# One turn of six raw weight tiles for all loads of the MLP, in place of two separate sets of three

## The chip, the cores and the metric

The kernel runs on one core of one Trainium2 chip. The metric is the device time of one execution in microseconds (us); lower is better. The core has a matrix engine (TensorE, PE in the rows; PEld is its weight load), three engines for elementwise work (VectorE or DVE, ScalarE or ACT, GpSimd or POOL), and SyncE (SP), which issues nearly all loads of this kernel in order from one queue.

## The reference

A two-layer decoder in float32 over 256 tokens, width 2048. Layer 1 is a sparse attention (an indexer picks 64 keys per query) and an MLP; layer 2 has a dilated-window attention over shared keys and values, and an MLP; a last RMSNorm follows. The part that this change touches most is the MLP, once in each layer:

```python
def sq_relu_mlp(h, w_up, w_down):      # w_up 2048 x 8192, w_down 8192 x 2048
    u = jax.nn.relu(h @ w_up)
    return (u * u) @ w_down
```

## The kernel before

Every float32 weight is used in two parts. `split` (line 188) makes them: ACT casts the raw block to a rounded high part `whi` (line 190), DVE subtracts to get the low part `wlo` (line 191), each 128x1024 in the MLP. A product is then three matmuls of 128x512 for each 128 rows (`mm3`, lines 194 to 196, or line 382 in `gemm`). There are five `whi` and five `wlo` buffers in the MLP.

The MLP walks over eight blocks of 1024 hidden columns, e = 0 to 7. `up(e)` computes a block of `h @ w_up`, `down(e)` adds that block's part of the second product to the residual. The order is up(0), up(1), down(0), up(2), down(1), and so on; "round e" below is up(e) with the down(e-1) behind it.

- `up(e)` multiplies most of the inner dimension by a scheme of seven products in place of eight (`seven`, line 720). It is called three times, and each call loads two raw tiles of 1 MB, `rx` and `ry`, that hold the blocks b11, b12 and b21, b22. A call is seven splits and four in-place DVE additions on the raw tiles (lines 719, 721, 723, 726: b11 = b12 - b11, b12 = b22 - b12, and so on). Line 721 is the first of the four that needs `ry`. `rx` is last read by the split of b12, `ry` by the split of b21, the last of the call. The rest of the inner dimension is two raw tiles, `rows[0]` and `rows[1]`, split in four ordinary products `plain(r, c)`: both of `rows[0]` are over in the middle of the second call of `seven`, those of `rows[1]` come at the end of the third call and behind it. Below, the three calls are the first, second and third seven, and the pair `rows` the plain rows.
- For e > 0 the plain rows are loaded behind the first seven's tiles; for e = 0 ahead of them.
- `down(e)` is two calls of `gemm`, each with four raw tiles of 1 MB: eight tiles, d0 to d7, two splits each.

So a round loads 16 tiles of 1 MB: six for the three sevens, two plain rows, eight of down. Before the change, the sevens' six take three buffers named `wx` (pool `mlp`), the other ten take three named `wraw` (pool `wp`, which also serves the attention stages). A tile takes the buffer of its pool and name that comes free first, and a buffer is free when its last reader is done. Each engine's order is written down when the kernel is built, by a scheduler that forecasts times; the loads stand on SP's one queue in that order, so one that waits for a buffer holds up those behind it. Between attention and MLP, `project` loads the output weights, and `add_forms` takes one such tile as scratch (`gx`) for each half.

Of the kernel before, what the change touches and what calls it, by code (L numbers as in the profile page):

```python
# [11 lines left out]
F32 = mybir.dt.float32  # L12
# [5 lines left out]
P = 128  # L18
SEQ = 256
NT = SEQ // P  # L20
D = 2048
KC = D // P
# [19 lines left out]
GW = 1024  # L42
# [9 lines left out]
X0 = 2  # L52
ARRIVE = 2

HI_BUFS, LO_BUFS = 4, 3
HI_MORE, LO_MORE, RAW_MORE = 1, 2, 3

Q_W = NH * HD
# [5 lines left out]
NSM = ID + IH  # L64
# [28 lines left out]
def yoco_kernel(ctx: ExitStack, tc: tile.TileContext, x, a_w_in, a_w_out, w_kv, b_w_q, b_w_out, w_up, w_down,  # L93
# [7 lines left out]
    wp = ctx.enter_context(tc.tile_pool(name="wp", bufs=3))  # L101
# [3 lines left out]
    pools = {}  # L105
# [20 lines left out]
    def b2(dt=F32):  # L126
        return wk.tile([P, 512], dt, name="b2" + ("r" if dt == F32R else ""), tag="b2", bufs=8)
# [7 lines left out]
    def side():  # L135
        return ps2.tile([P, HALF], F32, name="side")
# [51 lines left out]
    def split(hi, lo, src):  # L188

        nc.scalar.copy(hi, src)  # L190
        nc.vector.tensor_tensor(lo, src, hi.bitcast(F32), op=ALU.subtract)  # L191
# [6 lines left out]
    def mm_wide(acc, w_hi, w_lo, xk, first, last):  # L198

        def both():  # L200
            nc.tensor.matmul(acc, w_hi, xk.rearrange("p a t -> p (a t)"), start=first, stop=last)

        if not last:
            both()
        nc.tensor.matmul(acc[:, :SEQ], w_lo, xk[:, 0], start=False, stop=False)
        if last:
            both()
# [28 lines left out]
        lo = lo_of.tile([P, GW], F32R, name="wlo", bufs=LO_BUFS if lo_of is wp else LO_MORE)  # L236
        return hi, lo

    def pair_raw():
        return pools["mlp"].tile([P, 2, GW], F32, name="wx", bufs=RAW_MORE)  # L240

    def norm_transpose(c4, which):

# [40 lines left out]
    def add_forms(halves, half, which):  # L284
        n, plain, f = halves[half]

        def transposed(c, c2):
            pt = side().rearrange("p (c t) -> p c t", c=2)
            for j in range(2):
                cc = 2 * c2 + j  # L290
                for t in range(NT):
                    nc.tensor.transpose(pt[:, j, t * P:(t + 1) * P], h[t][c][:, cc * P:(cc + 1) * P], ident)
                g = which * KC + 4 * c + cc
                yield cc, pt[:, j, :], gT[:, g:g + 1]

        if plain is not None:
            for c in range(2):
                for cc, pt, g in transposed(2 * half + c, 1):
                    hi, lo = plain[:, 2 * c + cc - 2, 0, :], plain[:, 2 * c + cc - 2, 1, :]
                    nc.scalar.activation(hi, pt, AF.Copy, scale=g)  # L300
                    nc.vector.scalar_tensor_tensor(lo, pt, g, hi.bitcast(F32), op0=ALU.mult, op1=ALU.subtract)
        gx = pair_raw()[:, :, :n * SEQ].rearrange("p c (j t) -> p c j t", t=SEQ)
        for c in range(2):
            for c2 in range(n // 2):
                for cc, pt, g in transposed(2 * half + c, c2):
                    nc.scalar.activation(gx[:, c, cc], pt, AF.Copy, scale=g)
        a11, a21, a12, a22 = gx[:, 0, :, :P], gx[:, 0, :, P:], gx[:, 1, :, :P], gx[:, 1, :, P:]
        s1, s2, s3, s4 = (b2()[:, :n * P].rearrange("p (q t) -> p q t", t=P) for _ in range(4))
        nc.vector.tensor_tensor(s1, a21, a22, op=ALU.add)
        nc.vector.tensor_tensor(s2, a11, s1, op=ALU.subtract)  # L310
        nc.vector.tensor_tensor(s3, a11, a21, op=ALU.subtract)
        nc.vector.tensor_tensor(s4, a12, s2, op=ALU.add)
        for name, v in (("a11", a11), ("a12", a12), ("s4", s4), ("s1", s1), ("s3", s3), ("s2", s2), ("a22", a22)):
            split(f[name][:, :, 0], f[name][:, :, 1], v)
# [37 lines left out]
    def load_w(w, r0, nk, cols, width):  # L352

        n = len(cols) * width
        raw = wp.tile([P, 2, GW], F32, name="wraw", bufs=3).rearrange("p a b -> p (a b)")[:, :nk * n]
        raw = raw.rearrange("p (k c) -> p k c", k=nk)
        joined = all(c == cols[0] + i * width for i, c in enumerate(cols))
        for i, c in enumerate(cols[:1] if joined else cols):
            m = n if joined else width
            nc.sync.dma_start(raw[:, :, i * width:i * width + m],  # L360
                              w[r0:r0 + nk * P, c:c + m].rearrange("(k p) c -> p k c", p=P))
        return raw
# [69 lines left out]
    take_x(0, raw_x, 0, X0)  # L432
    stat = stat_of(xa)
    cols_qi = (COL_QI, COL_QI + HALF)
    raw_w = wp.tile([P, 2, GW], F32, name="wraw", bufs=3)
    for c in range(2):
        nc.sync.dma_start(raw_w[:, 0, c * HALF:(c + 1) * HALF], a_w_in[0, :P, cols_qi[c]:cols_qi[c] + HALF])
    take_x(0, raw_x, X0, 4)
# [21 lines left out]

    def index_keys():

        raw = wp.tile([P, 2, GW], F32, name="wraw", bufs=3).rearrange("p a b -> p (a b)")[:, :KC * NSM]
        nc.sync.dma_start(raw.rearrange("p (k n) -> p k n", n=NSM),
                          a_w_in[0, :, COL_KI:COL_KI + NSM].rearrange("(k p) c -> p k c", p=P))
        acc = ps.tile([P, HALF], F32, name="acc")[:NSM]
        per = KC // 2
        for k0 in range(0, KC, per):
            hi, lo = (b[:, :per * NSM] for b in hi_lo())
            split(hi, lo, raw[:, k0 * NSM:(k0 + per) * NSM])  # L470
            for k in range(k0, k0 + per):
                xk = xa[k // 4][:, k % 4]
                r = slice((k - k0) * NSM, (k - k0 + 1) * NSM)
                mm_wide(acc, hi[:, r], lo[:, r], xk, k == 0, k == KC - 1)
        both = sum_halves(acc)
        pt = side()
        for t in range(NT):
            nc.tensor.transpose(pt[:, t * P:t * P + NSM], both[:, t * P:(t + 1) * P], ident[:NSM, :NSM])
        rstd = st.inv()
        rk = wk.tile([P, NT], F32, name="rk", tag="rk", bufs=2)  # L480
        nc.vector.tensor_scalar(rk, rstd, -SCALE, None, op0=ALU.mult)
        rA.extend((rstd, rk))
        kps = side()
        for t in range(NT):
            r = rstd[:, t:t + 1]
            kk = wk.tile([P, P + 176], F32, name="kk", bufs=1)[:, :P]
            src = pt[:, t * P:t * P + NSM]
            nc.scalar.activation(kk[:, :ID], src[:, :ID], AF.Copy, scale=r)
            nc.vector.tensor_scalar(wi[t], src[:, ID:], r, r, op0=ALU.mult, op1=ALU.mult)
            nc.vector.tensor_scalar(wi[t], wi[t], WI_SCALE, None, op0=ALU.mult)  # L490
            rope(kk[:, :ID].unsqueeze(1), 1, RI // 2, t, True)
            nc.vector.tensor_copy(kk[:, ID:], kk[:, :ID])
            nc.tensor.transpose(kps[:, t * P:(t + 1) * P], kk, ident)
        split(kiT[:, 0], kiT[:, 1], kps[:, :SEQ])
# [171 lines left out]
    def mlp(i, xm, st_in, gains_next, final=None):  # L666
# [4 lines left out]
        def up(e):  # L671
# [8 lines left out]
            c0 = e * GW  # L680
            cl, cr = slice(0, HALF), slice(HALF, GW)

            def raws(k1, tile_of):
                out = []
                for k in (k1, k1 + 4):
                    r = tile_of()
                    nc.sync.dma_start(r, w_up[i][k * P:(k + 2) * P, c0:c0 + GW].rearrange("(k p) c -> p k c", p=P))
                    out.append(r)
                return out
# [13 lines left out]
            rows = []  # L703

            def plain_rows():
                rows[:] = raws(2, lambda: wp.tile([P, 2, GW], F32, name="wraw", bufs=3))

            def plain(r, c):
                f = xm[0][2]
# [3 lines left out]
            def seven(half, pair, within=lambda: None, before_last=lambda: None):  # L713

                f = {name: v[:, pair:pair + 2] for name, v in xm[half][2].items() if name[0] != "p"}
                rx, ry = raws(8 * half + pair, pair_raw)
                b11, b12, b21, b22 = rx[:, :, cl], rx[:, :, cr], ry[:, :, cl], ry[:, :, cr]
                product(b11, (f["a11"], "q1"))
                nc.vector.tensor_tensor(b11, b12, b11, op=sub)
                product(b21, (f["a12"], "q2"))  # L720
                nc.vector.tensor_tensor(b12, b22, b12, op=sub)  # L721
                product(b22, (f["s4"], "q3"))
                nc.vector.tensor_tensor(b22, b11, b22, op=sub)  # L723
                product(b11, (f["s1"], "q5"))
                within()
                nc.vector.tensor_tensor(b21, b21, b22, op=add)  # L726
                product(b12, (f["s3"], "q7"))
                product(b22, (f["s2"], "q6"))
                before_last()
                product(b21, (f["a22"], "q4"))  # L730
# [150 lines left out]
    def final(ustat, w, row0, r2):  # L881


        both = pair_raw().rearrange("p a c -> p (a c)")
        fg = [both[:, s * HALF:(s + 1) * HALF] for s in range(4)]
        for s in range(4):
            nc.scalar.dma_start(fg[s], final_norm[s * HALF:(s + 1) * HALF].partition_broadcast(P))
# [35 lines left out]
        nk = GW // P  # L923
# [7 lines left out]
        for k in range(nk):  # L931
            if k % 2 == 0:
                raw = load_w(w, row0 + k * P, 2, (GW, GW + HALF), HALF)
            if k < 6:
                both = new_xt().rearrange("p c a t -> p (c a t)")
# [18 lines left out]
        for i in range(2):  # L954
            c = slice(i * HALF // 2, (i + 1) * HALF // 2)
# [41 lines left out]
```

## Time and profile before

| | |
|---|---|
| median of 3 runs | 2268.68 us (2267.55 to 2270.04) |
| the profiled execution: its own time | 2272.53 us |
| the profiled execution: span from first to last instruction | 2270.7 us |
| mean granted TensorE clock | 0.984 of 2.4 GHz |
| PE busy | 2192.5 us (97%) |
| DVE busy | 1767.2 us (78%) |
| ACT busy | 1224.5 us (54%) |
| loads of 1 MB into `wraw` and `wx` in the MLPs | 128 of w_down, 96 and 32 of w_up |

The times of the three runs are device times; the profile is of one more execution, 3.85 us above their median. Idle time in the rows stands in brackets with what ended it ("[2.05 <-DMA wx<-in_w_up_dram]" is 2.05 us of idle time ended by a load). Spans of a few instructions of one kind are merged into one row with their count.

### The profile page before, as it was taken

The numbers are of one execution on the slowest core, as the hardware profiler recorded it, in microseconds if no ns is written. First come the engines' busy times: TensorE is split into PE (matmuls) and PEld (weight loads), VectorE is DVE, ScalarE is ACT, GpSimd is POOL, SyncE is SP. The second block draws the span as 40 slices with busy tenths as digits, with TensorE's granted clock in tenths as the row PEclk, the third lists the DMA queues.
The fourth block names the chain that finished last, engine by engine and source line by source line (L and its number), as shares of the span: only waits on it lengthen the run. The fifth ranks groups of instructions, "written<-read, shape, count | busy, mean of one in ns | idle before, by whom it ended". The sixth has DMA issues, their size and how long they took to land.

```text
span 2270.7 us, 27359 instructions
## 1 busy us (share of the span) xinstructions
PE 2192.5 (97%) x10310; PEld 1800.5 (79%) x10310; DVE 1767.2 (78%) x2379; ACT 1224.5 (54%) x1624; POOL 0.7 (0%) x6
## 2 busy tenths in 40 slices
PE   9999998999999999999999999998999999999998
PEld 7788876778787787788888888875787787787786
DVE  5877769887887978867577777769887978878775
ACT  6545556545645645546455555455645645556453
POOL 0000000000000000000000000000000000000000
PEclk9999999999999999999999999999999999999999
DMA  8554444646656456365554545554646456456453
GB/s 297 167 176 143 161 170 162 209 148 204 206 164 208 162 186 213 121 204 176 175 163 150 164 155 171 175 186 148 209 163 218 153 184 220 150 187 224 164 167 130
DMA packets 147974, 405.04 MB, mean 178 GB/s; under 512 B 11009, under 2 KB 60289, under 8 KB 147841
## 3 DMA queue, kind: packets, MB, share of 16 engines
q1 hardware_dynamic: 146688, 401.25, 53.4%
q10 hardware_dynamic: 1152, 2.04, 0.2%
q8 instruction: 81, 1.33, 0.2%
q14 instruction: 53, 0.43, 0.1%
HBM read 401.15 MB, written 2.10 MB: 178 GB/s over the span
## 4 chain that ended last, share of the span: by engine, by line
PE 72%; DVE 18%; DMA 6%; ACT 2%; issue 2%; SPq 0%; DVEq 0%; ACTq 0%
PE acc L382 56%; DVE wlo L191 10%; DMA wx<-in_w_up_dram 5%; PE side L393 2%; PE acc L194 2%; PE acc L195 2%; PE side L195 2%; PE acc L196 2%; PE side L196 2%; PE side L194 2%; DVE wx L723 2%; ACT whi L190 2%; DVE h L642 1%; DVE wx L726 1%; DVE wx L721 1%
## 5 line engine op out<-in xcount | busy, mean ns | idle before, releaser
L382 PE MATMUL acc<-whi,xt 128*128 128x512 f32 x4160 | 1106.9, 380 | 1.2 <-ACT whi L190 1.2
L190 ACT CAST whi<-wraw 128x1024 fp32r<-128x1024 f32 (+2 forms) x589 | 588.2, 1002 | 618.8 <-PE acc L382 445.3
L191 DVE TENSOR_TENSOR wlo<-wraw,whi 128x1024 fp32r<-128x1024 f32 (+2 forms) x589 | 678.0, 1161 | 307.2 <-ACT whi L190 186.9
L382 PEld LDWEIGHTS acc<-whi,xt 128*128 128x128 f32 x4160 | 738.1, 188 | 138.9 <-ACT whi L190 2.5
L382 PE MATMUL acc<-wlo,xt 128*128 128x512 f32 (+1 forms) x2080 | 618.7, 378 | 5.6 <-DVE wlo L191 5.6
L190 ACT CAST whi<-wx 128x1024 fp32r<-128x1024 f32 x336 | 343.0, 1050 | 323.8 <-DMA wx<-in_w_up_dram 114.0
L382 PEld LDWEIGHTS acc<-wlo,xt 128*128 128x128 f32 x2080 | 371.6, 188 | 79.6 <-DVE wlo L191 7.2
L191 DVE TENSOR_TENSOR wlo<-wx,whi 128x1024 fp32r<-128x1024 f32 x336 | 396.9, 1219 | 28.7 <-ACT whi L190 28.5
L194 PE MATMUL side<-whi,xt 128*128 128x512 f32 x320 | 129.3, 413 | 36.4 <-ACT whi L190 34.6
L194 PE MATMUL acc<-whi,xf 128*128 128x512 f32 x288 | 121.6, 423 | 13.2 <-ACT whi L190 12.9
L195 PE MATMUL side<-wlo,xt 128*128 128x512 f32 x320 | 131.8, 412 | 1.7 <-DVE wlo L191 1.7
L196 PE MATMUL side<-whi,xt 128*128 128x512 f32 x320 | 130.7, 409 | 0.0
L195 PE MATMUL acc<-wlo,xt 128*128 128x512 f32 x328 | 129.6, 395 | 1.0 <-DVE wlo L191 1.0
L194 PE MATMUL acc<-whi,xt 128*128 128x512 f32 x328 | 129.5, 399 | 0.5 <-ACT whi L190 0.5
L196 PE MATMUL acc<-whi,xt 128*128 128x512 f32 x328 | 129.1, 394 | 0.0
L195 PE MATMUL acc<-wlo,xf 128*128 128x512 f32 x288 | 117.2, 407 | 1.9 <-DVE wlo L191 1.9
L196 PE MATMUL acc<-whi,xf 128*128 128x512 f32 x288 | 115.5, 401 | 0.0
L194 PEld LDWEIGHTS side<-whi,xt 128*128 128x128 f32 x320 | 62.6, 196 | 58.8 <-ACT whi L190 43.9
L642 DVE SCALAR_TENSOR_TENSOR h<-acc,ri,h 128x512 f32<-128x512 f32 x127 | 86.6, 743 | 5.4 <-PE acc L196 5.4
L721 DVE TENSOR_TENSOR wx<-wx 128x1024 f32<-128x1024 f32 x48 | 58.8, 1225 | 36.9 <-DMA wx<-in_w_up_dram 35.9
L194 PEld LDWEIGHTS acc<-whi,xf 128*128 128x128 f32 x288 | 57.5, 200 | 37.3 <-ACT whi L190 26.1
L393 PE MATMUL side<-ident,b 128*128 128x128 f32 x512 | 77.1, 274 | 4.0 <-ACT b L761 3.5
(196 smaller groups left out, 1808.7 us busy)
## 6 DMA issues: line engine op xcount, KB each, us to landing
wraw<-in_w_down_dram SPq DMA_DIRECT2D x128, 1024.0 KB, 5.7
wx<-in_w_up_dram SPq DMA_DIRECT2D x96, 1024.0 KB, 5.2
wraw<-in_b_w_q_dram SPq DMA_DIRECT2D x192, 256.0 KB, 3.1
wraw<-in_w_up_dram SPq DMA_DIRECT2D x32, 1024.0 KB, 5.0
wraw<-in_a_w_in_dram SPq DMA_DIRECT2D x31, 1024.0 KB, 5.2
wraw<-in_a_w_out_dram SPq DMA_DIRECT2D x16, 1024.0 KB, 5.4
wraw<-in_b_w_out_dram SPq DMA_DIRECT2D x16, 1024.0 KB, 5.6
wraw<-in_w_kv_dram SPq DMA_DIRECT2D x8, 1024.0 KB, 5.0
```

The source lines that it names most:

```text
L190: nc.scalar.copy(hi, src)
L191: nc.vector.tensor_tensor(lo, src, hi.bitcast(F32), op=ALU.subtract)
L194: nc.tensor.matmul(o, a_hi, b_hi, start=start, stop=False)
L195: nc.tensor.matmul(o, a_hi, b_lo, start=False, stop=False)
L196: nc.tensor.matmul(o, a_lo, b_hi, start=False, stop=stop)
L382: nc.tensor.matmul(acc[t][i][:, :c1 - c0], stat(k, a, t), b[:, c0:c1], start=first and a == 0 and b is hi, stop=last and a == 1)
L393: nc.tensor.transpose(pt[:, j * P:(j + 1) * P], sr, ident)
L642: nc.vector.scalar_tensor_tensor(hh, acc, scale()[:, t:t + 1], hh, op0=ALU.mult, op1=ALU.add)
L721: nc.vector.tensor_tensor(b12, b22, b12, op=sub)
L723: nc.vector.tensor_tensor(b22, b11, b22, op=sub)
L726: nc.vector.tensor_tensor(b21, b21, b22, op=add)
```

## The change

All raw tiles of 1 MB are taken by one function, `raw_tile`. Outside the MLP it gives the three `wraw` buffers of pool `wp`, as before. While pool `mlp` is open (from the second part of `project` to the end of the MLP) it gives buffers in a turn of six: three from `wp`, then three from `mlp`. The sevens, the plain rows, the tiles of `gemm` and the scratch `gx` all share that turn. The memory is the same: three tiles in each pool. In `final`, the last gains `fg`, which took a `wx` tile, take the memory of the tile `xf4` (forms of the second half's activations, read by matmuls of the second and third seven).

```diff
-HI_BUFS, LO_BUFS = 4, 3
+HI_BUFS, LO_BUFS, RAW_BUFS = 4, 3, 3
 HI_MORE, LO_MORE, RAW_MORE = 1, 2, 3
@@
-    def pair_raw():
-        return pools["mlp"].tile([P, 2, GW], F32, name="wx", bufs=RAW_MORE)
+    raw_turn = [0]
+
+    def raw_tile():
+
+        of = wp
+        if "mlp" in pools:
+            of = wp if raw_turn[0] < RAW_BUFS else pools["mlp"]
+            raw_turn[0] = (raw_turn[0] + 1) % (RAW_BUFS + RAW_MORE)
+        return of.tile([P, 2, GW], F32, name="wraw", bufs=RAW_BUFS if of is wp else RAW_MORE)
@@ add_forms
-        gx = pair_raw()[:, :, :n * SEQ].rearrange("p c (j t) -> p c j t", t=SEQ)
+        gx = raw_tile()[:, :, :n * SEQ].rearrange("p c (j t) -> p c j t", t=SEQ)
@@ load_w
-        raw = wp.tile([P, 2, GW], F32, name="wraw", bufs=3).rearrange("p a b -> p (a b)")[:, :nk * n]
+        raw = raw_tile().rearrange("p a b -> p (a b)")[:, :nk * n]
@@ up: raws, plain_rows, seven
-            def raws(k1, tile_of):
+            def raws(k1):
                 out = []
                 for k in (k1, k1 + 4):
-                    r = tile_of()
+                    r = raw_tile()
...
-                rows[:] = raws(2, lambda: wp.tile([P, 2, GW], F32, name="wraw", bufs=3))
+                rows[:] = raws(2)
...
-                rx, ry = raws(8 * half + pair, pair_raw)
+                rx, ry = raws(8 * half + pair)
@@ final
-        both = pair_raw().rearrange("p a c -> p (a c)")
+        both = pools["mlp"].tile([P, 3 * GW], F32, name="fg", tag="xf4", bufs=1)
```

## Rows read from the trace of the kernel before

**Rows 1.** The page: busy time, share of the span and instructions of two engines, and the chain of work that ended last by engine.

```profile
PE 2192.5 (97%) x10310; PEld 1800.5 (79%) x10310; DVE 1767.2 (78%) x2379; ACT 1224.5 (54%) x1624; POOL 0.7 (0%) x6
PE 72%; DVE 18%; DMA 6%; ACT 2%; issue 2%; SPq 0%; DVEq 0%; ACTq 0%
```

**Rows 2.** Who waited for whom over the whole kernel: the waiting engine and line, what it waited for, us in total, times, the longest.

```profile
ACT whi L190 <- DMA wx<-in_w_up_dram: 114.0, 30, 7.5
DVE wx L721 <- DMA wx<-in_w_up_dram: 35.9, 16, 3.2
PE side L194 <- ACT whi L190: 34.6, 19, 3.7
PE acc L382 <- DVE wlo L191: 5.6, 6, 1.1
```

**Rows 3.** SP's queue over round 5 of the first layer, in order of time: start, us from the first to the last of the merged loads, the loads.

```profile
724.77 5.80 SPq L687 DMA_DIRECT2D wraw<-in_w_up_dram  x2
735.65 0.37 SPq L360 DMA_DIRECT2D wraw<-in_w_down_dram  x1
751.23 3.77 SPq L687 DMA_DIRECT2D wx<-in_w_up_dram  x2
763.97 0.37 SPq L360 DMA_DIRECT2D wraw<-in_w_down_dram  x1
766.24 18.52 SPq L687 DMA_DIRECT2D wx<-in_w_up_dram  x4
786.19 22.66 SPq L360 DMA_DIRECT2D wraw<-in_w_down_dram  x6
814.89 5.81 SPq L687 DMA_DIRECT2D wraw<-in_w_up_dram  x2
825.77 0.37 SPq L360 DMA_DIRECT2D wraw<-in_w_down_dram  x1
```

**Rows 4.** DVE in the same round: the first split of the first seven, then from the middle of the second seven to the last split of up.

```profile
737.12 1.23 DVE L191 TENSOR_TENSOR wlo<-wx,whi 128x1024 fp32r<-128x1024 f32 x1 [1.50 <-ACT whi L190]
...
762.73 1.22 DVE L191 TENSOR_TENSOR wlo<-wraw,whi 128x1024 fp32r<-128x1024 f32 x1
...
765.00 4.63 DVE L191 TENSOR_TENSOR wlo<-wx,whi 128x1024 fp32r<-128x1024 f32 x4
769.66 1.22 DVE L719 TENSOR_TENSOR wx<-wx 128x1024 f32<-128x1024 f32 x1
772.93 1.23 DVE L721 TENSOR_TENSOR wx<-wx 128x1024 f32<-128x1024 f32 x1 [2.05 <-DMA wx<-in_w_up_dram]
774.07 3.49 DVE L191 TENSOR_TENSOR wlo<-wx,whi 128x1024 fp32r<-128x1024 f32 x3
777.48 1.22 DVE L723 TENSOR_TENSOR wx<-wx 128x1024 f32<-128x1024 f32 x1
...
784.94 1.22 DVE L191 TENSOR_TENSOR wlo<-wraw,whi 128x1024 fp32r<-128x1024 f32 x1
```

**Rows 5.** The chain of work that ended last, its piece of this round that is a load.

```profile
766.24 6.59 DMA wx<-in_w_up_dram
```

**Rows 6.** PE in the same round, single matmuls at the start of the third seven, where the clock comes back, and at the end of up.

```profile
771.19 0.39 PE L194 MATMUL acc<-whi,xt 128*128 128x512 f32 x1
...
772.55 0.39 PE L194 MATMUL acc<-whi,xf 128*128 128x512 f32 x1
773.95 0.50 PE L194 MATMUL side<-whi,xt 128*128 128x512 f32 x1 [1.02 <-ACT whi L190]
...
779.54 0.41 PE L195 MATMUL acc<-wlo,xf 128*128 128x512 f32 x1
...
789.80 0.39 PE L196 MATMUL acc<-whi,xt 128*128 128x512 f32 x1
...
792.62 0.73 PE L382 MATMUL acc<-wlo,xt 128*128 128x512 f32 x2 [1.09 <-DVE wlo L191]
```

**Rows 7.** PE at the same place of round 2 of the first layer; from the first row to the last there are 16 matmuls.

```profile
501.85 0.39 PE L196 MATMUL acc<-whi,xt 128*128 128x512 f32 x1
...
510.25 0.40 PE L194 MATMUL acc<-whi,xf 128*128 128x512 f32 x1
```

**Rows 8.** Stretches of round 5: from:to, us, busy us of PE, PEld, DVE, ACT and POOL with their instructions, granted clock, DMA share, GB/s.

```profile
775.50:779.50 4.00, 4.00 (x11) 3.14 (x12) 4.00 (x4) 1.50 (x3) 0.00 (x0) 0.58 0.02 4
746.70:786.30 39.60, 38.13 (x159) 30.65 (x158) 37.45 (x36) 23.76 (x24) 0.00 (x0) 0.96 0.51 164
```

**Rows 9.** Round 0 of the first layer: DVE from the end of the second seven into the third; and of the page's loads, the median time from issue to landing of the sevens' tiles.

```profile
354.73 3.63 DVE L191 TENSOR_TENSOR wlo<-wx,whi 128x1024 fp32r<-128x1024 f32 x3
358.40 1.22 DVE L719 TENSOR_TENSOR wx<-wx 128x1024 f32<-128x1024 f32 x1
359.66 1.23 DVE L721 TENSOR_TENSOR wx<-wx 128x1024 f32<-128x1024 f32 x1
...
wx<-in_w_up_dram SPq DMA_DIRECT2D x96, 1024.0 KB, 5.2
```

**Rows 10.** Round 7 of the second layer, ACT and DVE in the third seven: the instruction that prepares the last norm's square root reads the gains `fg`.

```profile
2155.28 0.20 ACT L902 ACTIVATE root<-wx 128x1 f32<-128x1 f32 x1 [3.59 <-DMA wx<-in_final_norm_dram]
...
2156.45 3.50 DVE L191 TENSOR_TENSOR wlo<-wx,whi 128x1024 fp32r<-128x1024 f32 x3 [2.75 <-ACT whi L190]
```

More of the change, by code (lines that the diff above doesn't have):

```diff
@@ L434, in yoco_kernel @@
     cols_qi = (COL_QI, COL_QI + HALF)
-    raw_w = wp.tile([P, 2, GW], F32, name="wraw", bufs=3)
+    raw_w = raw_tile()
     for c in range(2):
@@ L461, in index_keys @@
     def index_keys():
-        raw = wp.tile([P, 2, GW], F32, name="wraw", bufs=3).rearrange("p a b -> p (a b)")[:, :KC * NSM]
+        raw = raw_tile().rearrange("p a b -> p (a b)")[:, :KC * NSM]
         nc.sync.dma_start(raw.rearrange("p (k n) -> p k n", n=NSM),
```

## The prediction

> **What bounds the kernel now.** I read the page first: PE is busy for 97% of the span and DVE for 78%, and yet the chain that ended last spends 18% on DVE and 6% in loads [rows 1]. A chain on PE alone would leave nothing for a change in loads. Next the waits: ACT's casts wait 114.0 us for the sevens' tiles, and DVE's addition on line 721, the first that needs `ry`, waits 35.9 us in 16 waits, about one in each round [rows 2]. Then one round in order of time, round 5 of the first layer. On SP's queue the last load that the third seven needs, its `ry`, is the first of the four at 766.24 [rows 3]; the chain holds it for 6.59 us [rows 5]. DVE finishes line 719 at 769.66 + 1.22 = 770.88 and stands until 772.93 [rows 4]. PE, which began the third seven at 771.19 and ran six matmuls in 1.36 us (0.227 us each), stands too [rows 6], and behind that its granted clock is 0.58, near the lower of its two levels, for some 4 us [rows 8]. From 772.55 to 779.54 it starts 14 matmuls: 6.99 - 14 x 0.227 = 3.8 us lost [rows 6]. In round 2 the same place costs 8.40 - 16 x 0.227 = 4.8 us [rows 7]. The other fact to see is how full DVE is: 37.45 of 39.60 us of up [rows 8], the hole of 2.05 us being nearly all it has. So up is bounded by DVE with a load in its way, and down by PE.
>
> **Why that load is late.** With three `wx` buffers, the third seven's `ry` needs the buffer of the second seven's `rx`. That is last read by the first of the four splits at 765.00, about 766.15, and the load goes out at 766.24 [rows 3, 4].
>
> **What the change does to the loads.** Rounds move 16 tiles, the turn is six, so three patterns of buffers repeat over the rounds. I wrote each out, giving a tile the first free buffer of its set of three.
> - The third seven. In rounds 1, 4, 7 its two tiles follow, in `wp`, the first seven's two and `rows[0]`; in rounds 2, 5 they follow, in `mlp`, the first seven's two and one of the second; in rounds 3, 6 `rx` follows the first seven's `rx` in one set, and `ry` the first seven's `ry` in the other. In all three, `rx` gets the buffer freed at 751.2 and `ry` the one freed at 754.6 (the two loads at 751.23 and 3.77 - 0.37 later are waits on just these releases [rows 3]). `ry` is then issued about 11.6 us earlier; with the same 6.59 us it lands at 761.2, 9.7 us ahead of line 721.
> - The second seven and the plain rows take buffers that down's later tiles leave. The last two of those are free at 820.3 and 825.8 (the end of the row at 814.89, and 825.77 [rows 3]), before up begins, and are needed well within it.
> - Down. d0 takes the buffer of `rows[0]` or of the second seven's `rx`, at 764 to 766, as now. Now d2 waits until 786.19 for `rows[1]`, which is held longest, and d3 to d7 for d0 to d4. After, one down tile still waits for `rows[1]` or the third seven's `ry`: d3, d2 or d1 by the pattern. The others go out sooner. The worst is d1, at 784.4 (the fourth load of the row at 766.24 [rows 3]): with 6.59 us it lands at 791.0, and PE, in down from 790.03, has d0 for 24 matmuls, 5.4 us. Its two splits just fit. I take 0 for down.
>
> **The sum.** Rounds 1 to 7 of both layers, 14 in all: the wait on line 721 goes. The two rounds 0 add next to nothing to the 35.9 us now, so the removed DVE time is 35 us [rows 2]. Is it worth that on the end? In round 5 everything behind 772.93 moves up by 2.05 us, and the last split of up ends at 784.94 + 1.22 - 2.05 = 784.1 [rows 4]. PE would still wait a little, because nine DVE steps of 1.14 us from 769.66 reach the sixth split at 779.95, where PE, five products of 1.36 us behind 771.19, wants it at 778.2. From 779.95, 35 matmuls of 0.227 us remain, so up ends at 787.9, not 790.03 (the last matmul begins at 789.80 [rows 6]): 2.1 us for 2.05. I take **-35 us**. Its bounds: no PE loss left at all, 14 x 4.3 (the mean of 3.8 and 4.8) = 60 us [rows 6, 7]; or, below, PE reaches down earlier and waits there for DVE's first low parts. That wait stands at 792.62 with 1.09 us and in six places [rows 2, 6]; if nine more rounds get it, at 1.4 us with the transposes, 13 us of the 35 go, leaving 22.
>
> Rounds 0 lose. There the plain rows come first, so the six tiles between them and the third seven's `ry` use up the turn. `rows[1]` is still held, so `ry` must wait for the second seven's `ry` instead of its `rx`, as now. That is last read by the second split at 354.73, until about 357.0 [rows 9]. DVE now goes from line 719 to 721 with no wait (358.40, 359.66 [rows 9]). After, the tile lands between 357.0 + 5.2 and 357.0 + 6.59, so line 721 waits 2.5 to 3.9 us [rows 5, 9]. I take 3.3, twice: **+6.6 us**. The Trainium skill's "SBUF — State Buffer", section "The DMA setup-cost knee", gives about 2 us plus the bytes at 436 GB/s, an estimate of 4.4 us for 1 MB: by it the wait would be 1.7 us and the term 3.4 us. The trace's 5.2 and 6.59 us disagree with it, and the term goes by them.
>
> Round 7 of the second layer: the square root's preparation, which DVE's hole let in, holds ACT for 3.59 us for `fg` and then DVE for 2.75 us [rows 10]. After, `fg` waits for `xf4`, so this moves behind up. It may hurt as much there or nothing: 0 to -2.8, I take **-1.4 us**. `gx` in the turn costs 0: its six buffers are all free by then, and the attention stages keep their three.
>
> Sum: -35 + 6.6 - 1.4 = -29.8 us. The profiled execution took 2272.53 us, so 2242.7; the runs' median is 3.85 us below it, so **2239 us**. Own range of this case: 2228 to 2250. Bounds: 60 - 5 + 2.8 = 58 us less is 2211; 22 - 7.8 = 14 us less is 2254.
>
> **Rivals.**
> - *PE recovers all of it* (0.10). The clock stays up, and the scheduler, which now forecasts `ry` early, moves splits of the plain rows forward. For: 3.8 to 4.8 us a round are lost [rows 6, 7]. Against: DVE's 37.45 of 39.60 us [rows 8]. Time 2268.7 - 56 = 2213.
> - *DVE takes the wait back* (0.16). The lateness of 1.75 us per third seven lowers the clock again, or the wait at the start of down appears in every round. Gain 12 to 20: about 2253.
> - *Nothing changes* (0.05). The written order keeps `ry` where it is on the queue, behind d1 at 763.97 [rows 3]: 2269.
> - *Slower* (0.07). `rows[1]` is held from before up to 786.2 [rows 4], and now shares buffers with the sevens. If the written order puts a load that waits for it ahead of the third seven's `ry`, that tile goes out at 786.19 and not 766.24, and the round loses 20 us. Two such rounds of the 14 use up the gain: 2279 at two, and slower from there.
>
> **Numbers.** The likeliest has 0.62. The range 2214 to 2258 runs from the full recovery to the case in which DVE takes most back. Faster 0.62 + 0.10 + 0.16 = 0.88, same 0.05, slower 0.07; 0.2% (4.5 us) is about what a measurement of this kernel can tell from no change.
>
> **What would show it.** Line 721 without a load in its waits in rounds 1 to 7, and 2.5 to 3.9 us in each round 0; ACT's 114 us of waits for the sevens' tiles mostly gone; third-seven loads on SP's queue some 16 us before their use; rounds of about 87.6 instead of 90.1 us; DVE without a hole in up. PE idle in the third seven should be pieces below 1 us that end on `whi` or `wlo`. The prediction is wrong if a load still ends the wait of line 721, if the time lost reappears at the start of down, or if the granted clock in the third seven still falls in most rounds.

## The result, and the profile after

| | before | after |
|---|---|---|
| median | 2268.68 us (2267.55 to 2276.59, 5 runs) | 2256.51 us (2256.02 to 2257.40, 5 runs) |
| ratio, 95% interval | | 0.9941 (0.9923 to 0.9958) |
| span of the profiled execution | 2270.7 us | 2254.2 us |

The change gains 12.2 us. Forecast were 2239 us, a gain of 29.8. The steady rounds gained more than that, and the way into each MLP lost more than half of it.

The page after, its busy times and the chain that ended last by engine:

```profile
PE 2179.4 (97%) x10310; PEld 1792.4 (80%) x10310; DVE 1762.1 (78%) x2379; ACT 1231.5 (55%) x1624; POOL 0.7 (0%) x6
...
PE 71%; DVE 22%; issue 4%; ACT 3%; DMA 1%; DVEq 0%; ACTq 0%
```

Against [rows 1] the loads have left the chain (6% to 1%), DVE has taken most of their share (18% to 22%).

The waits after (line numbers are seven higher than before from `gemm` on: line 721 is now 728):

```profile
...
ACT b L331 <- DVE h L647: 30.9, 4, 11.7
DVE h L647 <- PE acc L389: 29.9, 6, 9.7
...
DVE wraw L728 <- DMA wraw<-in_w_up_dram: 5.7, 2, 3.0
...
ACT whi L190 <- DMA wraw<-in_w_up_dram: 3.5, 2, 2.0
```

The two waits for loads of `w_up` that led [rows 2] are as good as gone: 114.0 us to 3.5, 35.9 to 5.7. Two that have no load in them have grown, to 30.9 and 29.9 us in four to six pieces of up to 11.7 us, where the same pairs came to 8.1 and 5.1 us before: a step of `project` in which ACT waits for DVE and DVE for PE.

From the first matmuls of each stage on PE one can draw up where the 16.5 us of the spans lie. The order ends with up(7), down(6), down(7), so the last of these stretches holds two downs.

| stretch | before, us | after, us | difference |
|---|---|---|---|
| start to down(0) of layer 1 | 429.4 | 443.0 | +13.5 |
| layer 1, up(2) to up(7) | 263.8 | 242.6 | -21.2 |
| layer 1, down(0) to down(5) | 276.8 | 279.6 | +2.8 |
| down(6) of layer 1 to down(0) of layer 2 | 661.4 | 672.9 | +11.5 |
| layer 2, up(2) to up(7) | 266.2 | 242.6 | -23.6 |
| layer 2, down(0) to down(5) | 275.4 | 275.6 | +0.2 |
| down(6) of layer 2 to the end | 97.7 | 97.9 | +0.2 |

The two stretches that lose hold `project`, up(0) and up(1). PE reaches up(0) 20.9 us later in each layer (in layer 2 from down(6) on), and up(0) and up(1) together then take 7.4 and 9.3 us less than before, so the 13.5 and 11.5 us are not the price of one stage. Two stages are worth looking at: a steady round, and `project` with round 0.

**A steady round.** Round 5 of layer 1, SP's two loads of the third seven, DVE in the third seven, then PE's only idle time there, then the whole of up(5) as a stretch with the columns of [rows 8]:

```profile
752.47 3.77 SPq L694 DMA_DIRECT2D wraw<-in_w_up_dram  x2
```
```profile
765.99 5.76 DVE L191 TENSOR_TENSOR wlo<-wraw,whi 128x1024 fp32r<-128x1024 f32 x5
771.66 1.21 DVE L726 TENSOR_TENSOR wraw<-wraw 128x1024 f32<-128x1024 f32 x1
772.80 1.22 DVE L191 TENSOR_TENSOR wlo<-wraw,whi 128x1024 fp32r<-128x1024 f32 x1
773.93 1.21 DVE L728 TENSOR_TENSOR wraw<-wraw 128x1024 f32<-128x1024 f32 x1
775.07 1.22 DVE L191 TENSOR_TENSOR wlo<-wraw,whi 128x1024 fp32r<-128x1024 f32 x1
776.21 1.22 DVE L730 TENSOR_TENSOR wraw<-wraw 128x1024 f32<-128x1024 f32 x1
```
```profile
778.61 0.50 PE L194 MATMUL acc<-whi,xf 128*128 128x512 f32 x1 [0.36 <-ACT whi L190]
```
```profile
747.95:788.15 40.20, 39.84 (x176) 32.51 (x175) 39.77 (x40) 27.37 (x28) 0.00 (x0) 1.00 0.56 186
```

The same stretch of before, from the first matmul of up(5) to the first of down(4), and DVE's second hole in it:

```profile
746.71:790.03 43.32, 41.85 (x176) 33.72 (x174) 40.18 (x40) 26.85 (x28) 0.00 (x0) 0.96 0.55 181
```
```profile
789.55 0.69 DVE L753 TENSOR_TENSOR b<-acc,b 128x512 f32<-128x512 f32 x1 [0.99 <-PE acc L196]
```

Four things are to be seen. No load ends a wait in the third seven: its `ry` went out at 752.47 + 3.77 - 0.37 = 755.87 and landed 5.2 us later, long before line 728 at 773.93. The granted clock is 1.00 over the whole up, where [rows 8] had 0.58 in 4 us of it. DVE is busy for 39.77 of 40.20 us, so up now lasts as long as DVE's work; PE, with 39.84 us, is as full. And DVE's order is another: before, both additions ran first and three splits behind them [rows 4]; now additions and splits take turns, and the split of b21, which needs only the raw `ry`, has gone ahead of the first addition into the group of five at 765.99.

**`project`.** The last step of layer 1's attention multiplies by the output weights in two halves, and `add_forms` stands behind each. ACT around the end of the first half, after:

```profile
281.53 1.05 ACT L190 CAST whi<-wraw 128x1024 fp32r<-128x1024 f32 x1 [1.23 <-PE acc L389]
294.23 0.63 ACT L331 ACTIVATE b<-h 128x512 f32<-128x512 f32 x1 [11.64 <-DVE h L647]
...
304.58 0.41 ACT L190 CAST xf<-b 128x256 fp32r<-128x256 f32 x1
304.89 4.83 ACT L190 CAST whi<-wraw 128x1024 fp32r<-128x1024 f32 x5
```

PE where the second half begins:

```profile
305.98 1.22 PE L389 MATMUL acc<-whi,xt 128*128 128x512 f32 x2 [3.85 <-ACT whi L190]
```

ACT before, in the same place:

```profile
289.67 1.05 ACT L190 CAST whi<-wraw 128x1024 fp32r<-128x1024 f32 x1 [1.66 <-PE acc L382]
292.39 1.06 ACT L190 CAST whi<-wraw 128x1024 fp32r<-128x1024 f32 x1 [1.67 <-PE acc L382]
295.11 1.05 ACT L190 CAST whi<-wraw 128x1024 fp32r<-128x1024 f32 x1 [1.66 <-PE acc L382]
296.06 0.63 ACT L324 ACTIVATE b<-h 128x512 f32<-128x512 f32 x1
```

Before, ACT goes on casting weights of the second half while PE finishes the first. After, it has cast all of the first half by 282.6, then stands for 11.64 us until that half's results are added, does `add_forms`, and only then casts five blocks in a row; PE waits 3.85 us for the first. SP's queue, loads of the output weights and the first of the MLP, after,

```profile
256.34 23.49 SPq L367 DMA_DIRECT2D wraw<-in_a_w_out_dram  x7
310.79 72.38 SPq L694 DMA_DIRECT2D wraw<-in_w_up_dram  x12
```

and, of the page's loads, the median time of the former from issue to landing:

```profile
wraw<-in_a_w_out_dram SPq DMA_DIRECT2D x16, 1024.0 KB, 5.6
```

All weights of the second half had been issued by 256.34 + 23.49 = 279.8. The seven loads of this row took 5.2 to 10.7 us to land, so the last was there by about 290.5, long before 304.89, when the first was cast: the casts stood behind `add_forms` in ACT's written order, not behind a load.

**Round 0.** DVE and PE in the third seven of layer 1's up(0), and the stretch behind it:

```profile
371.99 1.23 DVE L726 TENSOR_TENSOR wraw<-wraw 128x1024 f32<-128x1024 f32 x1
375.87 1.23 DVE L728 TENSOR_TENSOR wraw<-wraw 128x1024 f32<-128x1024 f32 x1 [2.66 <-DMA wraw<-in_w_up_dram]
```
```profile
376.95 0.50 PE L194 MATMUL side<-whi,xt 128*128 128x512 f32 x1 [3.20 <-ACT whi L190]
377.90 0.51 PE L194 MATMUL acc<-whi,xf 128*128 128x512 f32 x1 [0.45 <-ACT whi L190]
```
```profile
376.90:381.90 5.00, 4.50 (x11) 3.27 (x12) 5.00 (x6) 3.02 (x5) 0.00 (x0) 0.66 0.00 0
```

The stall moved here from the other rounds, as forecast, and has the forecast's size (2.66 and, in layer 2, 3.0 us). PE stands for 3.20 + 0.45 us, and behind it the granted clock is 0.66 for 5 us.

### The profile page after: what moved, and what is told of

Its sections match the earlier page's. It is cut to its first block, busy times and chain, and to the rows that moved or that the text cites. A ratio compares the mean times of both kernels' runs of the same rounds, so it can differ in the third digit from the quotient of the medians.

```text
span 2254.2 us, 27433 instructions
## 1 busy us (share of the span) xinstructions
PE 2179.4 (97%) x10310; PEld 1792.4 (80%) x10310; DVE 1762.1 (78%) x2379; ACT 1231.5 (55%) x1624; POOL 0.7 (0%) x6
## 4 chain that ended last, share of the span: by engine, by line
PE 71%; DVE 22%; issue 4%; ACT 3%; DMA 1%; DVEq 0%; ACTq 0%
PE acc L389 56%; DVE wlo L191 12%; PE side L400 2%; DVE wraw L730 2%; PE side L195 2%; PE side L196 2%; PE acc L195 2%; PE side L194 2%; PE acc L196 2%; PE acc L194 2%; DVE wraw L728 2%; DVE wraw L726 2%; DVE h L649 1%; ACT whi L190 1%; DVE wraw L733 1%
## 5 line engine op out<-in xcount | busy, mean ns | idle before, releaser
L190 ACT CAST whi<-wraw 128x1024 fp32r<-128x1024 f32 (+2 forms) x925 | 931.6, 1020 | 883.5 <-PE acc L389 564.7
L191 DVE TENSOR_TENSOR wlo<-wraw,whi 128x1024 fp32r<-128x1024 f32 (+2 forms) x925 | 1070.4, 1180 | 319.3 <-ACT whi L190 199.7
L389 PEld LDWEIGHTS acc<-whi,xt 128*128 128x128 f32 x4160 | 740.4, 189 | 148.4 <-ACT whi L190 10.7
L194 PE MATMUL side<-whi,xt 128*128 128x512 f32 x320 | 124.8, 400 | 15.4 <-ACT whi L190 14.6
L196 PE MATMUL side<-whi,xt 128*128 128x512 f32 x320 | 127.1, 397 | 0.0
L194 PE MATMUL acc<-whi,xf 128*128 128x512 f32 x288 | 116.0, 403 | 6.0 <-ACT whi L190 5.8
L196 PE MATMUL acc<-whi,xf 128*128 128x512 f32 x288 | 112.7, 391 | 0.0
L400 PEld LDWEIGHTS side<-ident,b 128*128 128x128 f32 x512 | 62.2, 140 | 25.3 <-ACT b L768 10.2
L194 PEld LDWEIGHTS acc<-whi,xt 128*128 128x128 f32 x328 | 61.8, 190 | 23.0 <-ACT whi L190 11.0
L195 PEld LDWEIGHTS side<-wlo,xt 128*128 128x128 f32 x320 | 61.6, 193 | 14.9 <-DVE wlo L191 2.0
```

Source lines behind the costliest of these rows:

```text
L194: nc.tensor.matmul(o, a_hi, b_hi, start=start, stop=False)
L195: nc.tensor.matmul(o, a_hi, b_lo, start=False, stop=False)
L196: nc.tensor.matmul(o, a_lo, b_hi, start=False, stop=stop)
L389: nc.tensor.matmul(acc[t][i][:, :c1 - c0], stat(k, a, t), b[:, c0:c1], start=first and a == 0 and b is hi, stop=last and a == 1)
L400: nc.tensor.transpose(pt[:, j * P:(j + 1) * P], sr, ident)
```

## The experiments

The theory after the result: the steady rounds gain what the late load cost; what is lost lies in `project`, because its weights and the scratch `gx` now share one turn, and in round 0. In the turn, the first half's `gx` comes ahead of one of the second half's weight tiles in pool `mlp`. The scheduler then expects that tile only when `gx` has been used, and writes the casts behind it. The rivals are that round 0 or the steady rounds account for the missing gain.

**e4: the suspected loss alone.** Kernel before, with the turn in `project` only; the MLP has `wraw` and `wx` as before.

```diff
+    raw_turn = [None]
+    def raw_tile():
+        of = wp
+        if raw_turn[0] is not None:
+            of = wp if raw_turn[0] < 3 else pools["mlp"]
+            raw_turn[0] = (raw_turn[0] + 1) % 6
+        return of.tile([P, 2, GW], F32, name="wraw" if of is wp else "wx", bufs=3)
@@ add_forms
-        gx = pair_raw()[:, :, :n * SEQ].rearrange("p c (j t) -> p c j t", t=SEQ)
+        gx = raw_tile()[:, :, :n * SEQ].rearrange("p c (j t) -> p c j t", t=SEQ)
@@ load_w
-        raw = wp.tile([P, 2, GW], F32, name="wraw", bufs=3).rearrange("p a b -> p (a b)")[:, :nk * n]
+        raw = raw_tile().rearrange("p a b -> p (a b)")[:, :nk * n]
@@ project, behind open_scope("mlp")
+        raw_turn[0] = 0
@@ mlp
+        raw_turn[0] = None
```

> The kernel before, with the turn of six for weights and gx in project alone; the MLP keeps its two sets of three. Theory A: 20 to 28 us slower than before, about 2293 us. Theory B: as before, about 2269 us.

Measured: 2293.24 us (2290.83 to 2296.46), ratio 1.0101 (1.0083 to 1.0119): 23 us slower than before by this part alone. ACT shows the same hole in the same place:

```profile
294.35 0.63 ACT L334 ACTIVATE b<-h 128x512 f32<-128x512 f32 x1 [11.64 <-DVE h L650]
```

**e1 and e2: the turn without `project`.** The changed kernel, with `project` as before (weights in `wp`, `gx` in pool `mlp`), the turn begun at up(0); e1 begins it with place 4, so that the steady rounds take the same buffers as in the changed kernel, e2 with place 0.

```diff
-    raw_turn = [0]
+    raw_turn = [None]
@@ raw_tile
-        if "mlp" in pools:
+        if raw_turn[0] is not None:
@@ add_forms
-        gx = raw_tile()[:, :, :n * SEQ].rearrange("p c (j t) -> p c j t", t=SEQ)
+        gx = pools["mlp"].tile([P, 2, GW], F32, name="wraw", bufs=RAW_MORE)[:, :, :n * SEQ].rearrange("p c (j t) -> p c j t", t=SEQ)
@@ mlp
+        raw_turn[0] = 4      # e2: 0
... (behind the last down: raw_turn[0] = None)
```

> The changed kernel, but the part of project ahead of each MLP is as before (weights in the three tiles of wp, the scratch gx straight from pool mlp); the turn of six starts at up(0), at its place 4, as in the changed kernel. Theory A (the shared turn in project pushes the second half's weight splits behind add_forms on ACT and DVE; 25 us over both layers): about 2231 us. Theory B (the 25 us sit in round 0, in the third seven's late tile, and in what follows it): no change, about 2256 us. By both, line 728 still waits 2.5 to 3.9 us for a load in round 0.

> As e1, but the turn starts at place 0 at up(0), so that the plain rows of round 0 lie in wp with the first seven's rx, and the third seven's two tiles follow in wp and need not wait for the second seven. Theory A: another 3 to 7 us below e1, about 2226 us, and no wait for a load on line 728 in round 0. Theory B: 25 us below e1, about 2231 us.

Measured: e1 2236.4 us (2235.17 to 2237.76), ratio 0.9850 (0.9835 to 0.9865); e2 2223.9 us (2222.99 to 2224.80), ratio 0.9795 (0.9780 to 0.9810). Both have the same up(2) to up(7) as the changed kernel (485.4 us over both layers, against 485.2). e2 has no wait on the second addition that ends on a load. So `project` was the loss. The place at which the turn begins decides another 12.5 us: e1 still has the stall of round 0 in both layers, 5.3 us in two waits, e2 has none. That price is not clean, since with place 4 the first tiles of up(0) also come behind `gx` in pool `mlp` (up(0) begins at 328.5 us in e1, at 320.3 in e2).

**e3: `gx` or the weights?** The changed kernel, with the turn kept for the weights of `project`; only the first half's `gx` stands elsewhere, in two tiles of 128x512.

```diff
-        gx = raw_tile()[:, :, :n * SEQ].rearrange("p c (j t) -> p c j t", t=SEQ)
+        if n == 2:
+            gx = [b2().rearrange("p (j t) -> p j t", t=SEQ) for _ in range(2)]
+        else:
+            both = raw_tile().rearrange("p c (j t) -> p c j t", t=SEQ)
+            gx = [both[:, c] for c in range(2)]
... (the uses of gx follow: gx[c][:, cc] for gx[:, c, cc], and so on)
@@ mlp
+        raw_turn[0] = 4
```

> The changed kernel with the shared turn kept for the weights of project; only the scratch gx of the first half is moved out of the raw tiles, into two 128x512 tiles of pool wk; the turn is set to place 4 at up(0) as in the changed kernel. Theory A1 (gx stands in the pool's order ahead of the next weight tile, and that alone shifts the splits): about 2231 us, as e1. Theory A2 (the turn itself does it, since its fourth tile lies in memory that the attention stage leaves late): about 2256 us.

Measured: 2230.16 us (2228.39 to 2231.41), ratio 0.9820 (0.9802 to 0.9838). One small scratch, moved, gives back 24.6 us of the span (2254.2 to 2229.6). ACT's hole has closed:

```profile
292.33 1.05 ACT L190 CAST whi<-wraw 128x1024 fp32r<-128x1024 f32 x1 [1.67 <-PE acc L393]
295.05 1.06 ACT L190 CAST whi<-wraw 128x1024 fp32r<-128x1024 f32 x1 [1.67 <-PE acc L393]
296.01 0.62 ACT L335 ACTIVATE b<-h 128x512 f32<-128x512 f32 x1
```

PE reaches up(0) at 319.0 us, as before the change, and with the same time from down(6) to up(0) of layer 2 (548.6 us against 548.7). So the weights in the turn cost nothing in `project`; the first half's `gx` ahead of one of them was all.

**e5: `gx` elsewhere and the turn from place 0.** e2 with e3's edit of `gx`; the second half's stays in pool `mlp`.

```diff
-        gx = pools["mlp"].tile([P, 2, GW], F32, name="wraw", bufs=RAW_MORE)[:, :, :n * SEQ].rearrange("p c (j t) -> p c j t", t=SEQ)
+        if n == 2:
+            gx = [b2().rearrange("p (j t) -> p j t", t=SEQ) for _ in range(2)]
+        else:
+            both = pools["mlp"].tile([P, 2, GW], F32, name="wraw", bufs=RAW_MORE).rearrange("p c (j t) -> p c j t", t=SEQ)
+            gx = [both[:, c] for c in range(2)]
... (the uses of gx follow, as in e3)
```

> The kernel of e2 (project's weights in wp as before, the turn from place 0 at up(0)), and the scratch gx of the first half in two tiles of 128x512 of the small pool, as in e3; the second half's gx stays in pool mlp. Theory A: a gx of the first half in pool mlp holds something behind it in every version, and without it project and round 0 shorten by what e3 gained over e1 (2236.4 - 2230.2 = 6 us over two layers): 2218. Rival B: that gain belonged to the turn for project's weights, which is not here: 2224, as e2. down(0) of the first layer begins at 422 to 423 by A, at 425.5 by B.

Measured: 2222.69 us (2222.37 to 2223.27), ratio 0.9784 (0.9770 to 0.9799). That is the rival's time, but not its place: down(0) of layer 1 began at 423.5, 2.0 us earlier than in e2 and nearer to theory A's 422 to 423 than to 425.5; the stretch to down(0) of layer 2 gave 0.9 back. Theory A's 6 us are not there; a part of them in layer 1 is. Against e3, whose up(0) begins at the same time (318.99 and 319.28 us) and has the stall of round 0, e5 reaches down(0) 5.8 us earlier in layer 1, and the stretch to down(0) of layer 2 is 5.9 us shorter (0.9 of it ahead of up(0)), where DVE's rows show a stall of 2.7 us in each. That is not the price of the stall alone: e8, below, has no stall either and reaches down(0) of layer 1 at 425.9, 2.4 us behind e5.

**e7 and e8: which load makes the steady gain?** The kernel before, with one tile of each round moved, and no turn: in e7 `ry` of the third seven comes from `wp`, in e8 `ry` of the second. With three `wx` tiles, e7 still has the second seven's `ry` wait for the first seven's `rx`; in e8 the third seven's two tiles inherit the first seven's buffers, so neither is late.

```diff
... (raws takes one or two makers of tiles; raw_of_wp makes one of wp's)
-                rx, ry = raws(8 * half + pair, pair_raw)
+                rx, ry = raws(8 * half + pair, pair_raw, raw_of_wp if pair else pair_raw)      # e7
+                rx, ry = raws(8 * half + pair, pair_raw, raw_of_wp if half and not pair else pair_raw)      # e8
```

> The kernel before with one thing changed: the ry tile of the third seven is taken from the three buffers of wp, not from the three of the sevens. Project, gx, fg and all other tiles are as before, and ry of the second seven still waits for rx of the first. up(2) to up(7) took 43.9 us each before and 40.4 in the changed kernel, 3.7 less, where 2.5 was forecast from the wait on line 721. Theory A: the late load of the third seven carries all of the 3.7 (its wait, the clock behind it, and the order of DVE that the scheduler writes with it); the wait of ACT's casts for ry of the second seven costs nothing: up(2) to up(7) 40.5 us each, 2268.7 - 14 x 3.6 = 2218. Rival B: the late ry of the second seven carries the 1.2 that the forecast missed: up(2) to up(7) about 41.7 us, 2268.7 - 14 x 2.5 = 2234.

> The kernel before with one thing changed: the ry tile of the second seven is taken from the three buffers of wp. The third seven's two tiles then take the buffers of the first seven's, so that both late loads of a round are early, with no turn of six. Theory A (e7) and rival B both give up(2) to up(7) about 40.5 us and 2218; by B this kernel is 16 us faster than e7, by A they are equal. A third, C: the turn itself matters, because ten of the sixteen tiles and now one more share three buffers and down's loads come later: the ups shorten, but the downs grow by more than 1 us each and the time stays above 2232.

(The twelve ups took 44.2 us each before, not 43.9; with 40.4 after, that gives the 3.7.)

Measured: e7 2235.42 us (2234.63 to 2236.04), ratio 0.9840 (0.9825 to 0.9854); e8 2220.06 us (2219.67 to 2220.31), ratio 0.9772 (0.9755 to 0.9788). e7 has B's time, but not for B's reason: its up(2) to up(7) take 489.2 us together, close to e8's 485.3 and A's figure, and its downs are 11.6 us longer. The waits of e7:

```profile
...
ACT whi L190 <- DMA wx<-in_w_up_dram: 43.2, 14, 4.1
...
ACT b L763 <- DVE b L753: 34.5, 16, 2.6
...
PE side L393 <- ACT b L764: 16.0, 8, 3.4
```

and those of e8:

```profile
...
PE side L393 <- ACT b L764: 3.5, 3, 1.9
...
ACT whi L190 <- DMA wx<-in_w_up_dram: 1.1, 1, 1.1
```

In e7 ACT finishes up's results later in some rounds, and PE, already in down, waits for them in its transposes: 16.0 us against 3.5. So the third seven's load carries 40.8 of the 44.7 us in the ups, and moving the second's `ry` in its place gives the other 3.9 us and 11.6 in the downs. That the late `ry` itself delays ACT is not shown: the kernel before has the same late tile and 3.5 us of these waits, and the changed kernel, e2 and e5 have no late `ry` in rounds 1 to 7 and 8.4, 9.9 and 9.6 us. C falls: e8 moves one tile, has no turn, and is the fastest kernel of the study, 52 us under the runs of before beside it and some 36 under the changed kernel.

**e9: is it DVE's order?** e8 with the old order in the third seven, by a small instruction that makes the splits of the raw `ry` wait for both additions.

```diff
-                product(b21, (f["a12"], "q2"))
                 nc.vector.tensor_tensor(b12, b22, b12, op=sub)
+                if pair:
+                    mid = ry[:, :, HALF - 1:HALF + 1]
+                    nc.vector.scalar_tensor_tensor(mid, b12[:, :, :2], 0.0, mid, op0=ALU.mult, op1=ALU.add)
+                product(b21, (f["a12"], "q2"))
```

> The kernel of e8 (2220.06 us, up(2) to up(7) 40.2 to 40.7 us each, no late load in a round) with the old order of DVE brought back in the third seven alone: b12 = b22 - b12 stands ahead of the product of b21, and a DVE instruction on 128x4 elements, which adds zero times b12 to the middle columns of ry, makes both splits of the raw ry wait for it. DVE then runs the two additions, three splits, an addition, and so on, as before the change and as the forecast assumed, with no load to wait for. Theory A: the forecast's 2.5 us a round was right for that order, and the missing 1.2 us of the measured 3.7 came from the order that the scheduler wrote anew (the split of b21 ahead of the two additions): up(2) to up(7) 41.5 to 42 us, 2220 + 14 x 1.2 plus some 0.1 to 0.3 us a round for the added instruction, 2236 to 2241. Rival B: the order is worth nothing, and the forecast only priced the wait too low: up(2) to up(7) 40.3 to 40.9, 2221 to 2225.

Measured: 2251.49 us (2250.28 to 2252.83), ratio 0.9919 (0.9902 to 0.9935), 31 us slower than e8 (33 by the two ratios) and more than either theory gave. up(2) to up(7) take 508.7 us, 1.95 more each. DVE in the third seven of round 5:

```profile
763.81 1.23 DVE L723 TENSOR_TENSOR wx<-wx 128x1024 f32<-128x1024 f32 x1
765.07 0.17 DVE L726 SCALAR_TENSOR_TENSOR wx<-wx 128x4 f32<-128x4 f32 x1
766.35 3.50 DVE L191 TENSOR_TENSOR wlo<-wx,whi 128x1024 fp32r<-128x1024 f32 x3 [1.11 <-ACT whi L190]
```

The instruction makes ACT's cast wait too, and DVE then waits 1.11 us for the cast, so 0.17 + 1.11 = 1.28 us of the 1.95 are the price of the experiment. If DVE's time counts one for one, 0.67 us a round is left for the order: B's zero is unlikely, but the run doesn't show the size by itself.

## Why the prediction was right and wrong, step by step

- *The late load and its cause*: right. Line 721's wait is gone in rounds 1 to 7, in round 5 `ry` goes out 7.92 us behind the start of up(5), as forecast (755.87 - 747.95; 754.63 - 746.71), the load no longer ends the chain, the clock stays at 1.00 in up(5), and e7 shows that this one tile carries nine tenths of the gain in up.
- *Rounds 1 to 7, -35 us*: the mechanism was right, the term too small. Twelve of the 14 ups gained 44.8 us, 3.7 each and not 2.5; the two rounds 1 gained another 7.2 by e8 against before. These 52 us are within the stated bound of 60. The step that failed in this term is "nine DVE steps of 1.14 us from 769.66 reach the sixth split", with PE 1.75 us late. It kept the old written order and slid it forward. (Its own figures give 778.0 for PE and not 778.2, so a lateness of 1.95 us.) The measured lateness is 0.36 us. Two things are behind it. The scheduler, expecting `ry` early, wrote b21's split ahead of the additions (what this alone is worth, 0.7 us by e9, is an estimate); and the late `ry` of the second seven, not costed, was worth 0.3 us in each up (e7 against e8). A row that was to be had would have said it: over the whole of up(5) before, 746.71 to 790.03, DVE was idle for 43.32 - 40.18 = 3.1 us, not for the 2.05 of its largest hole, and up is now as long as DVE's work. The prediction's stretch ended at 786.30, ahead of the second hole, 0.99 us until PE, itself late, was done. Over the twelve ups DVE's idle time was 38.8 us, so it too gives less than the 44.8.
- *Rounds 0, +6.6 us*: nearly right. The wait was forecast at 2.5 to 3.9 us and is 2.66 and 3.0. The Trainium skill's "SBUF — State Buffer", section "The DMA setup-cost knee", had stood beside it with an estimated wait of 1.7 us, which these two rows don't bear out. What the stall costs depends on what it is held against. e3 and e8 begin up(0) at the same time (319.0 and 319.4 us), neither has the late load in up(1), and only e3 has the stall: its down(0) of layer 1 comes 3.4 us later, and the stretch to down(0) of layer 2 is 4.2 us longer, 7.6 together. Against e5 it is 5.8 and 5.9, but there e5's own shorter rounds 0 are counted in. The rounds 0 of before have no stall, as e8's have none, so 7.6 is what to hold against the term.
- *"`gx` in the turn costs 0"*: this is the step that broke the forecast. It asked whether buffers were free on the chip, and they were; but with the scratch ahead of a weight tile in one pool, the scheduler wrote the splits of the second half behind `add_forms` (the order shows this; how it reckons is not on record). e4 shows the price alone (+23 us), e3 its removal (24.6 us of the span). Against that stand the 15.6 us that rounds 1 to 7 gave more than forecast (52.0 against 35 and 1.4): the measured gain is the difference of two misses.
- *The round*: up and down together took 90.2 us before in the mean of the twelve rounds of the ledger and take 86.7 after, where 87.6 was forecast.
- *Down, 0*: nearly right, +3.0 us in twelve downs, 2.6 of them in one of layer 1 (46.8 to 49.4 us). There PE's transposes wait for ACT, as in e7.
- *Round 7 of layer 2, -1.4 us*: up(7) there took 46.3 us before and 40.5 after. e8, which leaves `fg` in a `wx` tile, has 40.7: the hole let that wait in, and with the hole gone the move of `fg` is worth nothing that these runs show.
- *The sum checked*: to the two down(0) together, `gx` costs 24.7 us (the changed kernel against e3), the rounds 0 7.6 (e3 against e8), the rounds 1 -7.2 (e8 against before): 25.1 us, where the table has 13.5 + 11.5 = 25.0. These are steps of one chain of runs, so they had to add up. e4 is the check from outside: there the two down(0) come 11.4 and 9.0 us later, 20.3 together. The other 4.4 us appear only where the MLP takes the turn too. What makes them is not shown; in e1 the first tiles of up(0) come behind `gx`, as in the changed kernel, and its two down(0) come 2.9 and 2.4 us behind e3's.
- *The rivals*: that a chain of other waits would take the gain back was seen, at the wrong place. "DVE takes the wait back" named 2253 us, near the 2256.5 measured, but the wait at the start of down did not come in every round and DVE was not the reason. Full recovery came near in the ups alone, by the way that rival named, splits moved forward. The slower case, a load behind `rows[1]` on the queue, did not occur.

## What to carry to other kernels

When buffers are pooled into one turn, follow every user of the turn through the written order, scratch tiles of the stages before and behind included: a tile that is free on the chip can still hold up whatever the scheduler places behind it. Before pooling, ask for the one tile that is late: moving it alone (e7) was worth three times what the whole turn was, and moving the tile whose buffer makes two loads early (e8) four times. Price a late load by all the idle time of the fullest engine over the stage, not by the wait of one row; even that was 38.8 us here where 44.8 were gained. Say of a new stall what run its price is taken against: beside two runs without it, the same stall cost 7.6 and 11.7 us.

## What the runs showed that was not expected

A DVE wait of 2.7 us in round 0 of layer 1 delayed down(0) by more than itself, 3.4 us against e8 and 5.8 against e5. In the changed kernel PE stood for 3.65 us in two pieces, and the mean granted clock in the 5 us behind it was 0.66 of 2.4 GHz, between its two levels of 1.2 and 2.4 GHz. The same shape is in a long down of e7, down(4) of layer 1, where PE waited 2.34 us for a transpose's input and the mean granted clock over the 5 us around it was 0.84:

```profile
778.78 0.33 PE L393 MATMUL side<-ident,b 128*128 128x128 f32 x1 [2.34 <-ACT b L764]
```
```profile
775.80:780.80 5.00, 2.66 (x11) 2.01 (x10) 5.00 (x6) 4.65 (x7) 0.00 (x0) 0.84 0.52 182
```
